# A decoder block on one core: where the low halves of weights are made, and Silu in one operation

## The chip, the cores and the metric

The kernel runs on one core of a Trainium2 chip. The metric is the time of one execution on the device in microseconds (us). Before the change it is 1216.52 us, the median of three runs (1215.63 to 1218.12). A further execution was recorded by the hardware profiler; all rows of the trace come from that one.

## The reference

One layer, 1024 tokens, width 1024, everything float32. `x` is normalised and modulated, one big projection gives eight parts, two branches use them, and gates merge the branches:

```python
mod = jax.nn.silu(c) @ w_ada + b_ada
shift, scale, gate = jnp.split(mod, 3, axis=-1)
h = rms_norm(x, norm_gain) * (1.0 + scale[:, None, :]) + shift[:, None, :]
q, k, v, z_a, u, z_b, m_a, m_b = jnp.split(h @ w_in, offs, axis=-1)
attn = stick_breaking_attention(to_heads(q), to_heads(k), to_heads(v))
p_a = (attn * jax.nn.silu(z_a)) @ w_branch_a
pooled = multiscale_causal_pool(u, pool_w, pool_scale)
p_b = (pooled * jax.nn.silu(z_b)) @ w_branch_b
merged = jax.nn.sigmoid(m_a) * p_a + jax.nn.sigmoid(m_b) * p_b
return x + gate[:, None, :] * (merged @ w_out)      # then a last rms_norm
```

The attention has 16 heads of 64; its weights are products of sigmoids over the keys, not a softmax. The pooling takes trailing means over 2, 4, 8 and 16 tokens, minus the token itself. Silu is a number times its sigmoid. It occurs three times that matter here: on `z_b` (the pooling branch's gate), on `z_a`, and on `c`, whose product with the last third of `w_ada` gives the output gate.

## The kernel before

**Halves.** Every operand of a big matmul is split in two: a high half, rounded to the matmul's input format (a copy on ScalarE), and a low half, the difference (a subtraction, mostly on VectorE). A product of two operands is three matmuls: high by high, high by low, low by high. Making halves is therefore a large part of the work of ScalarE and VectorE. `split` (L119) and `load_w` (L134) load a weight tile and make both halves on arrival.

**Tiles of weights made ahead.** The last big stage, attention, projects 40 tiles of `w_in` (keys, queries, `z_a` of eight pairs of heads, and 16 tiles of the merge gates) in the order of the list `tiles`. The first `PLAIN` = 8 are split on arrival: ScalarE makes the high half, GpSimd the low half (VectorE for tile 4). For the other 32 the low half is made in earlier stages and kept in DRAM, in `wl_d`. That is `make_lo(pl, n, bufs, later)` (L147): for each of `n` tiles it takes a buffer `lraw` from pool `pl`, loads the weights into it (L154), copies the high half into the single buffer `lhi` on ScalarE (L157), subtracts it in place on VectorE (L158), and stores the buffer to `wl_d` (L159). The text calls one such step a low part. In attention `load_parts` (L167) loads such a tile twice, the weights and the stored low half, and ScalarE copies the high half (L174).

**Stages in order.**
1. Statistics of `x`, the modulation, the transposed and modulated input `hT`, and the projection `u` with the pooling map already multiplied in (matmuls named wm, ua, u), up to 128.6 us.
2. The values `v` (128.6 to 215.6 us): sixteen blocks of 24 matmuls; each result is split (L614, L615) and stored to `v_d` (L616). In the sequence of `u`, eight low parts; after each value block `LO_V` says how many more, ten in all, with the two steps of one apart by a block (`later`). Four of the eight pooling differences (`make_d`) are made here too.
3. The gate's stage (from 215.6 us): for each of eight tiles of `z_b`, two halves of 24 matmuls each (10.89 us a tile), then `silu`: ScalarE writes the sigmoid to `gb` (L668), VectorE multiplies it by `z_b` (L669) and by the pooling difference and its scale (L670). The sums `t1`, `t2` of parts of `gb` are taken (L674 to L677). Here the low parts by `LO_ZB`, four in all, and the output gate: `c` is spread to all partitions, ScalarE takes its sigmoid into `gjunk`, VectorE multiplies (L683), and for each of eight tiles of `w_gate` a load (L685) and a product with a sum (L686). Buffers `lraw`, three of them, serve the low parts, `gjunk` and `w_gate` in turn. All lie in pool `pb`, which is open for this stage and the next.
4. The seven products (to 396.9 us): `gb` times `w_branch_b` as a two by two block product with seven multiplications instead of eight, p1, p5, p6, p7, p4, p3, p2. Each takes two pairs of operands: a weight block `a` (loaded at L653, some of them sums of blocks) and a block of `gb` or of `t1`, `t2`, both split (L658 and L659, L646 and L647). The second load buffer `ar` and the results lie in pool `sums`. That pool opens when `diffs` closes, that is, on the space of the pooling differences, after the last of them has been read at L670. After each product `LO_PB` low parts, ten in all, with buffers in `pb`.
5. Attention with the forty projections between its steps (396.9 to about 1036 us), then `w_branch_a`, the merge and `w_out` to the end. Here the order of the matmuls is written out by hand and pinned. GpSimd masks the blocks on the diagonal (L936) for VectorE's running products (L938).

**What sets the order.** In stages 2 to 4 nothing is pinned. A planner places the instructions on each engine's queue, and the DMAs on SP's, by its own modelled times: an instruction may go ahead of others that stand before it in the program, as soon as its inputs and a free buffer allow. On the chip each queue then runs strictly in the planned order, and an instruction that waits holds all behind it. Weight tiles have two buffers for the loaded tile (`raw`) and two for its halves (`whl`); matmul results have eight PSUM banks.

Of the kernel before, what the change touches and what calls it, by code (L numbers as in the profile page):

```python
# [9 lines left out]
F32 = mybir.dt.float32  # L10
F32R = mybir.dt.float32r
AF = mybir.ActivationFunctionType
# [3 lines left out]
P = 128  # L16
D = 1024
# [16 lines left out]
NWT = 4  # L34


PLAIN = 8

MASKED = 4
LO_V = (1, 0, 1, 1, 0, 1, 1, 0)  # L40
LO_ZB = (0, 1, 0, 1, 0, 1, 0, 1)
LO_PB = (1, 2, 1, 2, 1, 2, 1)

DIFFS = {1: 0, 4: 1, 7: 2, 10: 3}
HD = 64
# [12 lines left out]
def block_kernel(ctx, tc, a, out):  # L58
    nc = tc.nc
    v, act, gp = nc.vector, nc.scalar, nc.gpsimd  # L60

    def pool(name, **kw):
        return tc.tile_pool(name=name, bufs=1, reuse_waits="tile", **kw)
# [9 lines left out]
    def bank(tag, name):  # L73
        return psp.tile([P, 512], F32, tag=tag, bufs=BANKS[tag], name=name)
# [3 lines left out]
    def any_bank(name):  # L78
        return bank(next(turns), name)
# [54 lines left out]
    def load_w(src, name, hi_eng, lo_eng):  # L134
        raw = wts.tile([P, KB, P], F32, tag="raw", bufs=2, name=name + "_raw")
        nc.sync.dma_start(raw.rearrange("p k c -> p (k c)"), src)
        return split(raw, [P, KB, P], wts, "whl", 2, hi_eng, lo_eng, name)
# [6 lines left out]
    tiles += gates  # L144
    early_lo = iter(range(PLAIN, len(tiles)))

    def make_lo(pl, n, bufs=3, later=False):  # L147

        rest = []
        for _ in range(n):  # L150
            i = next(early_lo)
            raw = pl.tile([P, D], F32, tag="lraw", bufs=bufs, name=f"l{i}_raw")
            hi = pl.tile([P, D], F32R, tag="lhi", bufs=1, name=f"l{i}_hi")
            nc.sync.dma_start(raw, a["w_in"][tiles[i]])  # L154

            def low(i=i, raw=raw, hi=hi):
                act.copy(hi, raw)  # L157
                v.tensor_sub(raw.bitcast(F32R), raw, hi.bitcast(F32))  # L158
                nc.sync.dma_start(wl_d[i], raw)  # L159

            if later:
                rest.append(low)
            else:
                low()
        return rest

    def load_parts(i, name):  # L167
        if i < PLAIN:
            return load_w(a["w_in"][tiles[i]], name, act, v if i == MASKED else gp)
        raw = wts.tile([P, KB, P], F32, tag="raw", bufs=2, name=name + "_raw")  # L170
        nc.sync.dma_start(raw.rearrange("p k c -> p (k c)"), a["w_in"][tiles[i]])
        hl = wts.tile([P, 2, KB, P], F32R, tag="whl", bufs=2, name=name)
        nc.sync.dma_start(hl[:, 1].rearrange("p k c -> p (k c)").bitcast(F32), wl_d[i])
        act.copy(hl[:, 0], raw)  # L174
        return hl[:, 0], hl[:, 1]
# [17 lines left out]
    def project(ct, name, use, he, le):  # L193
        whl = load_w(a["w_in"][ct], name, he, le)
        for sh in range(2):
            ps = any_bank(f"{name}_{sh}")
            mm3(ps, whl, (h_hi, h_lo), range(KB), hmov(sh))
            use(sh, ps)
# [18 lines left out]
    with pool("init") as init:  # L217
# [101 lines left out]
        wg, maps, halves = {}, {}, {}  # L319
# [223 lines left out]
        for i in range(NA, KB):  # L543
            ps = bank("pj", f"u{i}_0")
# [14 lines left out]
    def load_u(j):  # L559
        u = dif.tile([P, S + 16], F32, tag="u", bufs=2, name=f"u{j}")  # L560
        v.memset(u[:, S:], 0.0)
        nc.sync.dma_start(u[:, :S], u_d[j])
        return u

    def make_d(j, u):
        win = WINDOWS[j // 2]
        cur, n, step = u, S + 16, 1
        while step < win:
            nxt = dif.tile([P, S + 16], F32, tag="win", bufs=2, name=f"win{j}_{step}")
            n -= step  # L570
            v.tensor_add(nxt[:, :n], cur[:, :n], cur[:, step:step + n])
            cur, step = nxt, 2 * step
        t0 = S - win + 1
        d = dif.tile([P, S], F32, tag="d", bufs=5, name=f"d{j}")
        v.scalar_tensor_tensor(d[:, :t0], cur[:, :t0], 1.0 / win, u[:, :t0], ALU.mult, ALU.subtract)
        tl = dif.tile([P, 16], F32, tag="tl", bufs=2, name=f"tl{j}")
        v.tensor_mul(tl[:, :win - 1], cur[:, t0:S], invn[:, 16 - win + 1:])
        v.tensor_sub(d[:, t0:], tl[:, :win - 1], u[:, t0:S])
        dhls[j] = d


    with pool("vp") as vp:
# [6 lines left out]
        for i in reversed(range(KB)):  # L589
            ps = any_bank(f"u{i}_1")  # L590
# [9 lines left out]
        for hf in range(2):  # L600
            if hf == 0:
                wv.append([load_wv(1, k2) for k2 in range(4)])
            for sb in range(8):
                ss = slice(sb * P, (sb + 1) * P)
                ps = any_bank(f"v{sb}_{hf}")
# [14 lines left out]

                now, todo = todo, make_lo(vp, LO_V[sb], later=True)
                if 8 * hf + sb in DIFFS:
                    j = DIFFS[8 * hf + sb]
# [8 lines left out]
    pb = pbs.enter_context(pool("pb"))  # L632
# [6 lines left out]
    sg = pb.tile([P, D], F32, name="sg")  # L639
# [4 lines left out]
    def b_op(src, name):  # L644
        hl = pb.tile([P, 2, 2, 512], F32R, tag="bhl", bufs=3, name=name)
        act.copy(hl[:, 0], src)  # L646
        v.tensor_sub(hl[:, 1], src, hl[:, 0].bitcast(F32))  # L647
        return hl
# [7 lines left out]
    def a_op(src, name):  # L656
        hl = wts.tile([P, 2, 2, 512], F32R, tag="whl", bufs=2, name=name)
        act.copy(hl[:, 0], src)  # L658
        v.tensor_sub(hl[:, 1], src, hl[:, 0].bitcast(F32))  # L659
        return hl  # L660

    for j in range(KB):
        if j not in dhls:
            make_d(j, load_u(j))

        def silu(sh, ps):
            z = gb[:, j, sh * 512:sh * 512 + 512]
            act.activation(z, ps, AF.Sigmoid)  # L668
            v.tensor_mul(z, ps, z)  # L669
            v.scalar_tensor_tensor(z, dhls[j][:, sh * 512:sh * 512 + 512], psc_v[:, j:j + 1], z, ALU.mult, ALU.mult)  # L670

        project(CZB + j, f"wzb{j}", silu, act, v)
        if j < 4:
            v.tensor_sub(t1[:, j], gb[:, j, 512:], gb[:, j, :512])  # L674
        else:
            v.tensor_sub(t2[:, j - 4], gb[:, j, 512:], t1[:, j - 4])
            v.tensor_sub(gb[:, j - 4, 512:], gb[:, j, 512:], gb[:, j - 4, 512:])  # L677
        make_lo(pb, LO_ZB[j])
        if j == 0:
            nc.sync.dma_start(sg, a["c_row"].broadcast_to([P, D]))  # L680
            gjunk = pb.tile([P, D], F32, tag="lraw", bufs=3, name="gjunk")
            act.activation(gjunk, sg, AF.Sigmoid)
            v.tensor_mul(sg, sg, gjunk)  # L683
        wg = pb.tile([P, D], F32, tag="lraw", bufs=3, name=f"wg{j}")
        nc.sync.dma_start(wg, a["w_gate"][j])  # L685
        v.scalar_tensor_tensor(wg, wg, 1.0, sg, ALU.mult, ALU.mult, accum_out=gate[:, j:j + 1])  # L686
        del dhls[j]
# [4 lines left out]
    sums = pbs.enter_context(pool("sums", side="right"))  # L692
# [48 lines left out]
    def copied(tag, bufs, j, src):  # L741
        t = sums.tile([P, 512], F32, tag=tag, bufs=bufs, name=f"{tag}_{j}")
        act.copy(t, src)
        return t
# [5 lines left out]
    for n, (name, a_of, b_of) in enumerate(products):  # L750
        c = {"p5": "b", "p3": "b", "p2": "c"}.get(name, "a")
        if c not in chain:
            chain[c] = [bank((tb if c == "b" else ta)[j], f"{name}_{j}") for j in range(4)]
        ps = chain[c]
        for q in range(2):
            wl_, ml_ = a_op(a_of(q), f"{name}a{q}"), b_op(b_of(q), f"{name}b{q}")
            for j in range(4):
                for e in range(2):
                    for i, (w, m) in enumerate(((0, 0), (0, 1), (1, 0))):
                        mm(  # L760
                            ps[j], wl_[:, w, e, j * P:(j + 1) * P], ml_[:, m, e],
                            start=name in ("p1", "p5", "p2") and (q, e, i) == (0, 0, 0), stop=(q, e, i) == (1, 1, 2),
                                skip_group_check=True,
                        )
        for j in range(4):
            if name == "p1":
                keep["s1", j] = copied("s1", 4, j, ps[j])
            elif name == "p6":
                keep["s2", j] = copied("s2", 4, j, ps[j])
            elif name == "p7":  # L770
                out_b(j + 4, 1, added(copied("s3", 2, j, ps[j]), chain["b"][j]))
            elif name == "p4":
                out_b(j + 4, 0, copied("s4", 2, j, ps[j]))
            elif name == "p3":
                out_b(j, 1, added(keep["s2", j], ps[j]))
            elif name == "p2":
                out_b(j, 0, added(keep["s1", j], ps[j]))
        make_lo(pb, LO_PB[n])
    pbs.close()


# [295 lines left out]
    with pool("fin") as fin:  # L1077
# [14 lines left out]
        for sh in range(2):  # L1092
            sl = slice(sh * 512, sh * 512 + 512)
            ms = []
            for j in range(KB):
# [8 lines left out]
                ps = bank("pj", f"pa{sh}_{j}")  # L1104
                n = 0
# [12 lines left out]
            for i in range(4):  # L1118
# [8 lines left out]
                for c_, cl in enumerate(pieces):  # L1127
                    w_ = cl.stop - cl.start
                    ps = bank(("z", "tr")[c_ % 2], f"o{sb}_{c_}")[:, :w_]
                    n = 0  # L1130
# [85 lines left out]
```

## Time and profile before

| what | value |
|---|---|
| median of three runs | 1216.52 us (1215.63 to 1218.12) |
| the profiled execution | 1219.61 us |
| its span, first to last instruction | 1217.9 us |
| TensorE busy | 1194.0 us, 98% |
| VectorE busy | 796.7 us, 65% |
| ScalarE busy | 549.9 us, 45% |
| GpSimd busy | 167.9 us, 14% |
| moved by DMA | 212.39 MB |

How to read it: engines are PE (TensorE matmuls), PEld (its weight loads), DVE (VectorE), ACT (ScalarE), POOL (GpSimd) and SP (the queue that issues DMAs). A row of the timeline gives start, duration, engine, line, operation, the tile written and the tiles read, shape and count; in brackets stands how long the engine was idle before, and what ended that. A row of a group gives the count, the busy time, the mean in ns, and after the bar the idle time before such instructions and its causes. The chain of waits is followed back from the last instruction to what released it, step by step. A window's row gives each engine's busy time in that stretch, and then the granted clock of TensorE as a share of full speed.

### The profile page before, as it was taken

How to read it: one execution, taken by the hardware profiler on the slowest of the kernel's cores; microseconds unless marked ns; L12 is line 12 of the kernel's file. 1: busy time of each engine (PE TensorE's matmuls, PEld its weight loads, DVE VectorE, ACT ScalarE, POOL GpSimd, SP SyncE). 2: the span in 40 equal slices, each digit the busy share in tenths (PEclk: the TensorE clock that was granted, in tenths of full speed). 3: DMA queues.
4: the chain of work that ended last, by engine and by line, in shares of the span. 5: the costliest groups of instructions: out<-in, count | busy, mean ns of one | idle time of the engine just before them, and what ended most of it. 6: DMA issues, size and time to landing. Idle time of an engine off the chain costs nothing.

```text
span 1217.9 us, 16134 instructions
## 1 busy us (share of the span) xinstructions
PE 1194.0 (98%) x5698; PEld 995.8 (82%) x5698; DVE 796.7 (65%) x1088; ACT 549.9 (45%) x1020; POOL 167.9 (14%) x352
## 2 busy tenths in 40 slices
PE   8999999999699999999999999999999999999997
PEld 7888888887488888888888888888888888888886
DVE  5754591686675186777768678687777753795643
ACT  5564331332453255655656555555655653232211
POOL 1000000000000333222222221222221210000001
PEclk9999999999899999999999999999999999999999
DMA  9649994767735732343534325353353335985622
GB/s 350 259 168 360 308 380 169 231 221 166 271 138 178 224 92 70 107 135 104 162 116 138 101 95 164 110 155 99 110 143 100 96 123 173 352 273 168 208 72 84
DMA packets 85699, 212.39 MB, mean 174 GB/s; under 512 B 10609, under 2 KB 24049, under 8 KB 83442
## 3 DMA queue, kind: packets, MB, share of 16 engines
q1 hardware_dynamic: 77410, 196.47, 49.8%
q10 hardware_dynamic: 8208, 14.88, 3.3%
q8 instruction: 45, 0.74, 0.3%
q14 instruction: 36, 0.29, 0.1%
HBM read 144.20 MB, written 50.34 MB: 160 GB/s over the span
## 4 chain that ended last, share of the span: by engine, by line
PE 82%; DMA 7%; DVE 5%; issue 4%; ACT 1%; POOL 0%; SPq 0%; POOLq 0%; ACTq 0%; DVEq 0%
PE p L108 38%; PE v L108 7%; PE o L108 6%; PE z L108 6%; PE av L108 5%; PE wt L108 5%; PE pa L108 5%; PE u L108 4%; DMA wl_d<-l_raw 3%; PE ua L108 3%; DMA l_raw<-in_w_in 1%; PE wm L108 1%; DMA m<-sb_d 1%; PE wzb L108 1%; DMA kh<-kh 1%
## 5 line engine op out<-in xcount | busy, mean ns | idle before, releaser
L108 PE MATMUL p<-hT,w 128*128 128x512 f32 x1920 | 480.1, 391 | 0.6 <-ACT m_sg L203 0.6
L108 PEld LDWEIGHTS p<-hT,w 128*128 128x128 f32 x1920 | 355.2, 188 | 74.8 <-ACT m_sg L203 1.0
L938 DVE TENSOR_TENSOR_SCAN om<-om 128x512 f32<-128x512 f32 (+7 forms) x128 | 175.7, 1373 | 124.7 <-ACT om L931 69.1
L931 ACT ACTIVATE om<-z 128x512 f32<-128x512 f32 (+2 forms) x192 | 94.5, 492 | 156.4 <-PE z L108 133.9
L957 ACT CAST wt<-wt 128x512 fp32r<-128x512 f32 (+1 forms) x160 | 88.2, 551 | 48.2 <-PE wt L108 47.9
L958 DVE TENSOR_TENSOR wt<-wt,wt 128x512 fp32r<-128x512 f32 (+1 forms) x160 | 99.2, 620 | 16.2 <-ACT wt L957 15.6
L108 PE MATMUL av<-wt,vv 128*128 128x512 f32 x320 | 106.4, 414 | 0.0
L936 POOL TENSOR_SCALAR_AFFINE_SELECT om<-om 128x128 f32<-128x128 f32 x128 | 56.4, 441 | 346.9 <-ACT om L931 287.5
L108 DVE TENSOR_TENSOR be<-be,om 128x511 f32<-128x511 f32 (+7 forms) x128 | 95.1, 748 | 1.1 <-POOL be L936 0.7
L932 ACT ACTIVATE be<-z 128x512 f32<-128x512 f32 (+2 forms) x192 | 94.1, 490 | 0.0
L108 PE MATMUL pa<-ga,wa 128*128 128x512 f32 x384 | 89.9, 390 | 0.7 <-DVE s L1110 0.6
L108 PE MATMUL o<-wo,mhl 128*128 128x512 f32 (+1 forms) x408 | 89.6, 377 | 0.0
L108 PE MATMUL wzb<-hT,wzb 128*128 128x512 f32 x384 | 87.6, 390 | 2.0 <-DVE wzb L123 2.0
L108 PE MATMUL wt<-ident,be 128*128 128x128 f32 x576 | 89.4, 273 | 0.0
L108 PE MATMUL v<-wv,hT 128*128 128x512 f32 x384 | 87.2, 389 | 0.0
L108 PEld LDWEIGHTS wzb<-hT,wzb 128*128 128x128 f32 x384 | 71.9, 188 | 17.5 <-DVE wzb L123 2.5
L108 PEld LDWEIGHTS pa<-ga,wa 128*128 128x128 f32 x384 | 71.9, 188 | 16.4 <-issue 1.0
L108 PEld LDWEIGHTS o<-wo,mhl 128*128 128x128 f32 x408 | 73.5, 188 | 14.1
L108 PEld LDWEIGHTS v<-wv,hT 128*128 128x128 f32 x384 | 72.1, 188 | 14.9
L108 PEld LDWEIGHTS wt<-ident,be 128*128 128x128 f32 x576 | 70.2, 141 | 11.6
L157 ACT CAST l_hi<-l_raw 128x1024 fp32r<-128x1024 f32 x32 | 33.6, 1051 | 72.6 <-DMA l_raw<-in_w_in 54.8
L158 DVE TENSOR_TENSOR l_raw<-l_raw,l_hi 128x1024 fp32r<-128x1024 f32 x32 | 39.1, 1222 | 41.7 <-ACT l_hi L157 41.6
(175 smaller groups left out, 1481.8 us busy)
## 6 DMA issues: line engine op xcount, KB each, us to landing
w_raw<-in_w_in SPq DMA_DIRECT2D x40, 512.0 KB, 4.6
l_raw<-in_w_in SPq DMA_DIRECT2D x32, 512.0 KB, 4.9
wl_d<-l_raw SPq DMA_DIRECT2D x32, 512.0 KB, 5.9
w<-wl_d SPq DMA_DIRECT2D x32, 512.0 KB, 4.0
v_d<-vo SPq DMA_DIRECT2D x16, 512.0 KB, 5.2
vv<-v_d SPq DMA_DIRECT2D x8, 1024.0 KB, 5.3
wa_raw<-in_w_branch_a SPq DMA_DIRECT2D x16, 512.0 KB, 4.8
wa<-in_w_mod SPq DMA_DIRECT2D x7, 1024.0 KB, 6.3
```

Of the source, the lines that this page charges most:

```text
L108: ins = op(*args, **kw)
L157: act.copy(hi, raw)
L158: v.tensor_sub(raw.bitcast(F32R), raw, hi.bitcast(F32))
L931: act.activation(om[:, b0:b0 + n], zp[:, :n], AF.Sigmoid, scale=-0.125)
L932: act.activation(be[:, b0:b0 + n], zp[:, :n], AF.Sigmoid, scale=0.125)
L936: gp.affine_select(out=tl[:, :P], in_=tl[:, :P], pattern=[[1, P]], compare_op=ALU.is_gt, fill=fill, base=0, channel_multiplier=-1)
L938: v.tensor_tensor_scan(om[:, :W], om[:, :W], om[:, :W], 1.0, ALU.mult, ALU.min)
L957: act.copy(wt[:, 0, :off], pt[:, :off])
L958: v.tensor_sub(wt[:, 1, :off], pt[:, :off], wt[:, 0, :off].bitcast(F32))
```

## The change

Three things. First, the low parts: `PLAIN` goes from 8 to 10, so that 30 low parts are left; the values' blocks take 14 instead of 10, the gate's stage none instead of 4, the products 8 instead of 10. The products' low parts get their buffers in `sums`, two instead of three `lraw`. Second, `w_gate` gets one buffer of its own, `wg`, in place of a turn in `lraw`. Third, ScalarE writes Silu itself, of `z_b` and of `c`, and VectorE's multiplications at L669 and L683 go.

```diff
-PLAIN = 8
+PLAIN = 10
...
-LO_V = (1, 0, 1, 1, 0, 1, 1, 0)
-LO_ZB = (0, 1, 0, 1, 0, 1, 0, 1)
-LO_PB = (1, 2, 1, 2, 1, 2, 1)
+LO_V = (1, 1, 1, 1, 1, 1, 1, 0)
+LO_PB = (0, 2, 1, 2, 1, 1, 1)
...
             z = gb[:, j, sh * 512:sh * 512 + 512]
-            act.activation(z, ps, AF.Sigmoid)
-            v.tensor_mul(z, ps, z)
+            act.activation(z, ps, AF.Silu)
             v.scalar_tensor_tensor(z, dhls[j][:, sh * 512:sh * 512 + 512], psc_v[:, j:j + 1], z, ALU.mult, ALU.mult)
...
-        make_lo(pb, LO_ZB[j])
         if j == 0:
             nc.sync.dma_start(sg, a["c_row"].broadcast_to([P, D]))
-            gjunk = pb.tile([P, D], F32, tag="lraw", bufs=3, name="gjunk")
-            act.activation(gjunk, sg, AF.Sigmoid)
-            v.tensor_mul(sg, sg, gjunk)
-        wg = pb.tile([P, D], F32, tag="lraw", bufs=3, name=f"wg{j}")
+            act.activation(sg, sg, AF.Silu)
+        wg = pb.tile([P, D], F32, tag="wg", bufs=1, name=f"wg{j}")
         nc.sync.dma_start(wg, a["w_gate"][j])
...
-        make_lo(pb, LO_PB[n])
+        make_lo(sums, LO_PB[n], 2)
```

## The prediction

> **What bounds the kernel now.** I read the page first, then the waits of TensorE, its timeline around the one place where it stands still, the windows there, and the chain that ended last.
>
> ```profile
> span 1217.9 us, 16134 instructions
> ```
> ```profile
> 294.38 10.73 PE L108 MATMUL wzb<-hT,wzb 128*128 128x512 f32 x46 [2.04 <-DVE wzb L123]
> 310.05 1.22 PE L108 MATMUL p<-p1b,p1a 128*128 128x512 f32 x2 [4.94 <-ACT p1a L658]
> 311.61 6.71 PE L108 MATMUL p<-p1b,p1a 128*128 128x512 f32 x22 [0.34 <-DVE p1a L659]
> 321.88 7.22 PE L108 MATMUL p<-p1b,p1a 128*128 128x512 f32 x24 [3.56 <-ACT p1a L658]
> 330.85 11.28 PE L108 MATMUL p<-p5b,p5a 128*128 128x512 f32 x48 [1.74 <-ACT p5a L658]
> 341.97 11.15 PE L108 MATMUL p<-p6b,p6a 128*128 128x512 f32 x48
> 352.95 11.15 PE L108 MATMUL p<-p7b,p7a 128*128 128x512 f32 x48
> ...
> 396.90 25.37 PE L108 MATMUL p<-hT,w 128*128 128x512 f32 x111
> ```
> ```profile
> 190.00:200.00 10.00, 10.00 (x46) 8.29 (x45) 0.71 (x2) 1.18 (x2) 0.00 (x0) 1.00 0.31 111
> ...
> 290.00:300.00 10.00, 7.96 (x35) 6.09 (x35) 7.85 (x10) 3.10 (x5) 0.00 (x0) 1.00 0.67 190
> 300.00:310.00 10.00, 5.11 (x23) 3.91 (x21) 3.29 (x4) 3.52 (x4) 0.00 (x0) 0.89 0.84 286
> 310.00:320.00 10.00, 7.93 (x24) 5.61 (x24) 7.32 (x9) 3.24 (x4) 0.00 (x0) 0.77 0.92 338
> 320.00:330.00 10.00, 7.22 (x24) 5.50 (x24) 7.28 (x8) 4.20 (x7) 0.00 (x0) 0.83 0.62 236
> ...
> 440.00:460.00 20.00, 20.00 (x104) 16.90 (x103) 17.91 (x22) 12.83 (x27) 5.92 (x11) 1.00 0.45 105
> ```
> The columns of a window are TensorE, its weight loads, VectorE, ScalarE, GpSimd, the granted clock, the share of the DMA engines and GB/s. TensorE is full in the values' stage (190) and in attention (440); between 292 and 331 it waits five times, 2.04 + 4.94 + 0.34 + 3.56 + 1.74 = 12.62 us. Besides, the clock fell to 0.89, 0.77 and 0.83 there: 0.51 of 10 us is 5.1 us of clock withheld, part of it while TensorE stood idle anyway.
>
> What the place costs in all follows from the pitch of the work. The chain has the start of the gate's stage and, further on, what held it:
> ```profile
> 215.64 10.89 PE wzb L108 x48
> ...
> 271.70 13.11 DMA wl_d<-l_raw
> 284.83 4.17 DMA l_raw<-in_w_in
> ```
> A gate tile takes 10.89 us, a product 352.95 - 341.97 = 10.98. Eight tiles from 215.64 end at 302.76, seven products at 379.62. The projections start at 396.90, so **17.28 us** are lost in the two stages, by idleness and clock together. That is the most that the change can win here, and elsewhere TensorE has no wait worth naming.
>
> The cause stands on ScalarE:
> ```profile
> 307.52 1.04 ACT L157 CAST l_hi<-l_raw 128x1024 fp32r<-128x1024 f32 x1 [4.96 <-DMA l_raw<-in_w_in]
> 308.48 0.59 ACT L668 ACTIVATE gb<-wzb 128x512 f32<-128x512 f32 x1
> 308.96 1.03 ACT L658 CAST p1a<-a 128x1024 fp32r<-128x1024 f32 x1
> ```
> ```profile
> L157 ACT CAST l_hi<-l_raw 128x1024 fp32r<-128x1024 f32 x7 | 7.3, 1048 | 32.1 <-DMA l_raw<-in_w_in 29.4 <-DVE wzb L123 2.8
> L668 ACT ACTIVATE gb<-wzb 128x512 f32<-128x512 f32 x5 | 3.0, 590 | 0.0
> ```
> The second fence groups 285 to 325 us. ScalarE runs its queue in order. The copy of a low part (L157) waits 4.96 us for its weights; behind it stand the gate's sigmoid and p1's operand, for which TensorE waits 4.94. Seven such copies wait 32.1 us. Their weights are late because a buffer comes free only when its low part has been stored: the chain's 13.11 us store, then the next load.
>
> **The change, part by part.**
>
> *Low parts out of the gate's stage.* The planner may run a low part ahead of its place in the program as soon as a buffer is there.
> ```profile
> L158 DVE TENSOR_TENSOR l_raw<-l_raw,l_hi 128x1024 fp32r<-128x1024 f32 x14 | 17.1, 1220 | 22.4 <-ACT l_hi L157 22.4
> ...
> L669 DVE TENSOR_TENSOR gb<-wzb,gb 128x512 f32<-128x512 f32 x16 | 10.9, 682 | 5.2 <-ACT gb L668 5.2
> ```
> From 215 to 335 all fourteen low parts of the two stages ran, the products' ten among them: their buffers lay in a pool that was open from the gate's first tile. Now four go to the values, two are dropped, and the eight left use a pool that opens only when the pooling differences have been read, so nothing can be drawn ahead into the gate's stage. With them go each one's load and store from SP's queue. All of the 17.28 us stood behind them: minus 17.28.
>
> *Four more in the values' stage.* Each brings 1.05 us on ScalarE, 1.22 on VectorE, a load and a store. The row at 190 shows 0.71 of 10 us of VectorE and 0.31 of the DMA engines used, and TensorE can run on over eight PSUM banks of 5.44 us. Cover enough: 0. Without it each costs at most a copy's mean wait, 32.1/7 = 4.6 us.
>
> *Eight in the products.* A cycle of a buffer is load, copy, subtraction, store:
> ```profile
> l_raw<-in_w_in SPq DMA_DIRECT2D x32, 512.0 KB, 4.9
> wl_d<-l_raw SPq DMA_DIRECT2D x32, 512.0 KB, 5.9
> ```
> 4.9 + 1.05 + 1.22 + 5.9 = 13.1 us, by two buffers one low part in 6.5 us; eight need 52 of the products' 77 us. But a copy that waits holds the operand copies behind it:
> ```profile
> 347.66 1.05 ACT L658 CAST p7a<-a11d 128x1024 fp32r<-128x1024 f32 x1 [3.50 <-PE p L108]
> ```
> This operand could begin at 347.66, its low half ends 1.05 + 1.22 later at 349.93, and p7 starts at 352.95: a cover of 3.0 us. A copy's wait of 4.6 exceeds it by 1.6. Two such operands fall into a product's 11 us, and a wait hurts if it begins in the last 1.6 us ahead of one: 8 x 2 x 1.6/11 = 2.3 of the eight. I take two at the full 1.6: **plus 3.2 us**. Bounds: 0, and all eight, 12.8. Gaps this short should leave the clock alone: the wait of 2.04 us at 294 left it at 1.00.
>
> *p1 to p5.* p5's second operand is loaded only after the last difference is read:
> ```profile
> 323.31 0.74 DVE L670 SCALAR_TENSOR_TENSOR gb<-d,vecs,gb 128x512 f32<-128x512 f32 x1
> ```
> From there to p5's start at 330.85 is 7.54 us. Afterwards this read comes about 302.76 + 0.59 = 303.35, p5 can start at 310.89, and p1 keeps TensorE until 313.74: hidden, with 2.85 us to spare.
>
> *Silu in one operation.* It takes sixteen multiplications of 0.68 us and one of 1.22 off VectorE, 12.1 us, and shortens the way from PSUM to p5. No Silu stands in the trace; the nearest row is the sigmoid at 0.59 us, and ScalarE is busy 4.20 of 10 us at most in the windows above, so double would be hidden as well, and half would gain nothing: 0. It needs another table than the sigmoid. A table change in this trace:
> ```profile
> 12.10 1.28 ACT L108 ACT_TABLE_LOAD   x1
> 13.39 1.09 ACT L108 ACTIVATE sigb<-crow 128x512 f32<-128x512 f32 x2
> ```
> 1.28 us, and the sigmoid follows within 0.01. Two changes are added, at the gate's start and here:
> ```profile
> 423.20 0.60 ACT L931 ACTIVATE om<-z 128x512 f32<-128x512 f32 x1 [2.76 <-PE z L108]
> ```
> ScalarE idles 2.76 us ahead of the first sigmoid of attention, so both are hidden: 0; uncovered, 2.6. The Trainium skill (ScalarE: Activation LUTs, "What ACT_TABLE_LOAD costs") counts about 2.66 us a change, with a drain of 1.38 that this trace does not show, and advises against mixing sets; by it the uncovered cost is 5.3, and covered, which 2.76 just allows, it is 0 too.
>
> *Two more plain tiles.* Tiles 8 and 9 (pair 2's query tile and a gate tile) get their low part from GpSimd during attention, and two loads, two copies and two stores vanish:
> ```profile
> 448.62 2.40 POOL L123 TENSOR_TENSOR w<-w_raw,w 128x1024 fp32r<-128x1024 f32 x1 [6.03 <-ACT w L128]
> 450.97 0.30 POOL L936 TENSOR_SCALAR_AFFINE_SELECT om<-om 128x128 f32<-128x128 f32 x1
> ```
> 2.40 us twice on GpSimd; the mask behind it started at once, and TensorE is full in that window (20.00 of 20). 0; uncovered, 4.8.
>
> *w_gate's own single buffer.* SP holds a load until the previous product has read the buffer. A turn is some 4.9 + 1.22 = 6.1 us of the tile's 10.89: 0.
>
> **Sum.** -17.28 + 3.2 = -14.1. The profiled execution, 1219.61 us (span 1217.9 and 1.7 around it), becomes 1205.5. It lay 3.1 above the median of the three runs; from the median 1216.52 comes **1202.4 us**. The best case, from the fastest run 1215.63 with no rest, is 1198.3; with all eight copies at the full rest of 12.8, 1212.0.
>
> **The rivals.**
>
> *The wait moves to p5.* Two low parts' loads get ahead of p5's in SP's queue as the new pool opens: 2 x 4.9 - 2.85 = 6.95 us, with the clock in the present ratio (17.28/12.62 = 1.37) 9.5, so 1208.7. The Trainium skill (TensorE: Matmul & The Clock Gate, "The HAM clock gate") has the clock fall to half after an idle window of 3.4 us and stay there for as long; by that two gaps of about 3.5 would add 1.7 each, 10.4 in place of 9.5. For it: both share queue and pool, and p5's own wait of 1.74 was a load's. Against: in the program they stand behind p5.
>
> *Slower: ScalarE's blockade moves whole into the products.* There too the low parts may be drawn together, now over two buffers instead of three, right behind p1. At the present price of 17.28/7 = 2.47 each, eight cost 19.8 us: 1216.5 - 17.3 + 19.8 = 1219.0. It decides once the copies wait 3.0 + 2.2 = 5.2 us on average, as two of the present did. Against it: 52 us of cycle in 77, and DMA engines no longer shared with the gate's loads.
>
> *No change: SP's queue was the cause.* If w_gate's single buffer holds the queue more than 10.89 - 6.1 = 4.8 us a tile, the gate's weights and p1's operands behind it come as late as now: 1216.5. Against: VectorE loses 12.1 us of multiplications and fourteen subtractions, and reads at once.
>
> **How the numbers follow.** The forecast, with a rest of 0 to 6 us, 0.67; the wait at p5 0.17; no change 0.09; slower 0.07. Three runs spread over 0.2%, so that is what a measurement can tell from none. Faster is 0.67 + 0.17 = 0.84. The range 1198.3 to 1212.0 holds the first two, some 0.83.
>
> **What would show it.** Right: between the gate's start and the first projection some 167 us instead of 181; no low part's subtraction between 216 and 303, four more before; two more table loads; VectorE's busy time down by about 14.5 us, GpSimd's up by 4.8; clock 1.00 at 300 to 330. Wrong: operand copies of p5 or p6 behind waiting low-part copies, TensorE idle over 6 us in the products, or its first projection later than 390 us.

## The result and the profile after

The changed kernel takes 1205.39 us (median of four runs, 1204.15 to 1206.92), the kernel before 1216.41 beside it. The ratio is 0.991, with a 95% interval of 0.9894 to 0.9925: 11.0 us faster, where 14.1 were forecast. The profiled execution took 1204.15 us, the fastest of the four, with a span of 1202.4; that of the kernel before, 1219.61, lay above all of its other executions there. So the two profiles lie further apart (15.5 us of span) than the medians.

The page of the changed kernel, busy times:

```profile
span 1202.4 us, 16106 instructions
...
PE 1189.3 (99%) x5698; PEld 993.1 (83%) x5698; DVE 786.8 (65%) x1069; ACT 550.5 (46%) x1020; POOL 172.2 (14%) x354
```

TensorE's timeline of the changed kernel from the end of the gate's stage to the first projection (the changed file is shorter, so that its line numbers are one lower than before up to the gate's stage and five lower behind it):

```profile
283.62 18.52 PE L107 MATMUL wzb<-hT,wzb 128*128 128x512 f32 x81
301.98 11.17 PE L107 MATMUL p<-p1b,p1a 128*128 128x512 f32 x48
312.99 7.49 PE L107 MATMUL p<-p5b,p5a 128*128 128x512 f32 x32
...
334.96 11.15 PE L107 MATMUL p<-p7b,p7a 128*128 128x512 f32 x48
347.83 3.95 PE L107 MATMUL p<-p4b,p4a 128*128 128x512 f32 x16 [1.72 <-ACT s L738]
352.07 7.67 PE L107 MATMUL p<-p4b,p4a 128*128 128x512 f32 x32 [0.29 <-DVE p4a L658]
360.44 11.28 PE L107 MATMUL p<-p3b,p3a 128*128 128x512 f32 x48 [0.70 <-ACT p3a L657]
371.56 11.15 PE L107 MATMUL p<-p2b,p2a 128*128 128x512 f32 x48
382.54 25.70 PE L107 MATMUL p<-hT,w 128*128 128x512 f32 x111
```

The waits of 2.04, 4.94, 3.56 and 1.74 us ahead of p1 and p5 are gone. New ones of 1.72, 0.29 and 0.70 stand at p4 and p3. The first projection starts at 382.54 instead of 396.90. The clock stays up (windows of the changed kernel, same columns as before):

```profile
300.00:310.00 10.00, 10.00 (x45) 8.21 (x44) 6.76 (x8) 3.85 (x5) 0.00 (x0) 1.00 0.64 234
310.00:320.00 10.00, 10.00 (x45) 8.22 (x44) 8.44 (x9) 7.06 (x10) 0.00 (x0) 1.00 0.86 305
320.00:330.00 10.00, 10.00 (x46) 8.19 (x45) 10.00 (x10) 5.02 (x6) 0.00 (x0) 1.00 0.74 249
```

What is left comes from ScalarE (timeline of the changed kernel):

```profile
346.25 1.04 ACT L156 CAST l_hi<-l_raw 128x1024 fp32r<-128x1024 f32 x1 [3.36 <-DMA l_raw<-in_w_in]
347.20 1.07 ACT L738 COPY s<-p 128x512 f32<-128x512 f32 x2
...
353.32 2.20 ACT L738 COPY s<-p 128x512 f32<-128x512 f32 x4 [0.86 <-DMA pb_d<-s]
358.85 0.59 ACT L738 COPY s<-p 128x512 f32<-128x512 f32 x1 [3.33 <-DMA pb_d<-s]
359.33 1.05 ACT L657 CAST p3a<-a12s 128x1024 fp32r<-128x1024 f32 x1
```

A low part's copy waits 3.36 us for its weights, and behind it stand the copies that empty p7's banks, for which p4 waits. Then ScalarE waits 3.33 us for a result buffer that has not been stored, and p3's operand stands behind that.

### The profile page after: what moved, and what is told of

It reads as the page before. It is cut to its first block, busy times and chain, and to the rows that moved or that the text cites. A ratio compares the mean times of both kernels' runs of the same rounds, so it can differ in the third digit from the quotient of the medians.

```text
span 1202.4 us, 16106 instructions
## 1 busy us (share of the span) xinstructions
PE 1189.3 (99%) x5698; PEld 993.1 (83%) x5698; DVE 786.8 (65%) x1069; ACT 550.5 (46%) x1020; POOL 172.2 (14%) x354
## 4 chain that ended last, share of the span: by engine, by line
PE 93%; DMA 3%; DVE 1%; issue 1%; ACT 1%; SPq 0%; POOL 0%; POOLq 0%; ACTq 0%; DVEq 0%
PE p L107 41%; PE wzb L107 7%; PE v L107 7%; PE pa L107 7%; PE o L107 6%; PE z L107 6%; PE av L107 6%; PE wt L107 5%; PE u L107 5%; PE ua L107 3%; DMA wa<-in_w_mod 1%; PE wm L107 1%; DMA wt<-in_w_ut 1%; DMA pb_d<-s 1%; DMA wl_d<-l_raw 0%
## 5 line engine op out<-in xcount | busy, mean ns | idle before, releaser
L933 DVE TENSOR_TENSOR_SCAN om<-om 128x512 f32<-128x512 f32 (+7 forms) x128 | 177.5, 1387 | 124.9 <-ACT om L926 69.0
L107 PEld LDWEIGHTS o<-wo,mhl 128*128 128x128 f32 x408 | 73.5, 188 | 14.1
L122 POOL TENSOR_TENSOR w<-w_raw,w 128x1024 fp32r<-128x1024 f32 x9 | 22.2, 2465 | 345.9 <-ACT w L127 345.9
L107 PE MATMUL z<-kl,q 128*128 128x512 f32 (+2 forms) x192 | 65.5, 341 | 0.0
```

The source lines that it names most:

```text
L107: ins = op(*args, **kw)
L122: lo_eng.tensor_tensor(lo, src, hi.bitcast(F32), op=ALU.subtract)
L933: v.tensor_tensor_scan(om[:, :W], om[:, :W], om[:, :W], 1.0, ALU.mult, ALU.min)
```

## The experiments

The theory at first (A): the low parts that the planner drew into the gate's stage held ScalarE, and with it TensorE. The rivals were B (VectorE's relief by Silu made the gain) and C (buffers shared with `w_gate`). Twelve runs were made in three groups, each group beside the kernel before, which gave 1216.3, 1217.6 and 1217.2 us.

**e1, the low parts alone.** The changed kernel, with the old way of Silu:

```diff
-            act.activation(z, ps, AF.Silu)
+            act.activation(z, ps, AF.Sigmoid)
+            v.tensor_mul(z, ps, z)
```

(`c` goes back to sigmoid and multiplication in the same way; its sigmoid takes the buffer `wg`.)

> The changed kernel with the sigmoid and the multiplications as before (ScalarE writes the sigmoid, VectorE multiplies, 16 x 0.68 + 1.22 = 12.1 us of VectorE put back); c's sigmoid goes into the one buffer of w_gate. Theory A, the low parts that were drawn into the gate's stage held ScalarE and with it TensorE: all of the gain stays, 1204 to 1207 us, from the gate's start to the first projection some 167 to 168 us as in the changed kernel (167.4), no second pair of table loads. Rival B, VectorE's relief made the gain: it falls away, 1211 us or more, that stretch 173 us or more.

Measured: 1207.82 us, ratio 0.9927 (0.9915 to 0.9939). The first projection starts at 383.56. Most of the gain is there without Silu. It is slightly above the range expected; its interval overlaps the changed kernel's.

**e2, Silu alone.**

```diff
-            act.activation(z, ps, AF.Sigmoid)
-            v.tensor_mul(z, ps, z)
+            act.activation(z, ps, AF.Silu)
```

(The same for `c`.)

> The kernel before with Silu in one operation alone; low parts and buffers as before. Theory A: nothing to measure, 1214.5 to 1217 us, TensorE still waits over 9 us for p1's operands (12.6 before in all). Rival B, VectorE at 10 of 10 from 230 to 280 delayed the low parts, so that its relief of 12.1 us frees the stage: 1205 to 1210 us.

Measured: 1207.26 us, ratio 0.9922 (0.991 to 0.9934). Theory A as stated is wrong: with all fourteen low parts at their old places in the program, Silu alone takes 9.0 us. TensorE's timeline of this kernel:

```profile
293.32 0.73 PE L108 MATMUL wzb<-hT,wzb 128*128 128x512 f32 x2 [1.53 <-ACT wzb L128]
294.95 10.74 PE L108 MATMUL wzb<-hT,wzb 128*128 128x512 f32 x46 [0.90 <-DVE wzb L123]
305.52 0.62 PE L108 MATMUL p<-p1b,p1a 128*128 128x512 f32 x2
306.91 7.14 PE L108 MATMUL p<-p1b,p1a 128*128 128x512 f32 x30 [0.76 <-DVE p1a L659]
```

But B alone does not stand either, since e1 does without Silu. Two edits that each bring nearly the whole are not two causes; they shorten the same thing. The candidate is the end of the series of low parts. Of the subtractions (line, engine, operation, count, durations in ns, start of the first and of the last) the kernel before and e2 have:

```profile
L158 DVE TENSOR_TENSOR l_raw<-l_raw,l_hi x32: 1200/1225/1227, 93.5 to 320.4; 128x1024 fp32r<-128x1024 f32 x32
```
```profile
L158 DVE TENSOR_TENSOR l_raw<-l_raw,l_hi x32: 1214/1224/1227, 93.5 to 309.2; 128x1024 fp32r<-128x1024 f32 x32
```

The last one comes 11.2 us earlier, about what Silu takes off VectorE (12.1); against another execution of the kernel before (316.6, e8 below) it is 7.4. VectorE was nearly full where the series ran (windows of the kernel before, columns as in the prediction):

```profile
230.00:240.00 10.00, 10.00 (x46) 8.29 (x45) 10.00 (x15) 4.13 (x5) 0.00 (x0) 1.00 0.85 287
240.00:250.00 10.00, 10.00 (x46) 8.29 (x45) 7.37 (x10) 0.96 (x2) 0.00 (x0) 1.00 0.59 203
250.00:260.00 10.00, 10.00 (x46) 8.29 (x45) 9.28 (x14) 4.58 (x7) 0.00 (x0) 1.00 0.76 273
260.00:270.00 10.00, 10.00 (x46) 8.29 (x45) 10.00 (x14) 4.53 (x6) 0.00 (x0) 1.00 0.60 206
270.00:280.00 10.00, 10.00 (x46) 8.29 (x45) 10.00 (x13) 3.78 (x5) 0.00 (x0) 1.00 0.96 143
```

That VectorE's relief is what moved the series is argued from this, not shown apart: with Silu the planner also put ScalarE's and SP's instructions of this stage in another order.

The gate's stage ends at 302.7. In the kernel before, ScalarE's copy of p1's second operand stands right behind the last low part's (320.80 behind 319.36), so that p1 cannot go on until the series is through. A late low part ahead of 302.7 costs little (here 1.53 + 0.90 us for a weight tile of the gate), one behind it holds TensorE.

**e3, drawing ahead allowed again.** The changed kernel with the products' low parts in the pool that is open from the gate's stage on:

```diff
-        make_lo(sums, LO_PB[n], 2)
+        make_lo(pb, LO_PB[n], 2)
```

> The changed kernel with one thing undone: the products' eight low parts take their two buffers from the pool that is open from the gate's stage on, so that the planner can draw them ahead. Theory A1, the stage broke because there were more low parts than buffer turns: eight by 13.1/2 us are 52 us, done by about 275 of 302, no wait there and none later in the products: 1201 to 1205 us. Theory A2, low parts in the gate's stage hold its ScalarE whatever their number: 8/14 of the 17.3 us lost come back, 1211 to 1214 us.

Measured: 1201.60 us, ratio 0.9878 (0.9866 to 0.9891), 3.8 us less than the changed kernel. The series and TensorE's first projection in this kernel:

```profile
L157 DVE TENSOR_TENSOR l_raw<-l_raw,l_hi x30: 1215/1224/1227, 94.5 to 271.1; 128x1024 fp32r<-128x1024 f32 x30
```
```profile
379.67 20.61 PE L107 MATMUL p<-hT,w 128*128 128x512 f32 x90
```

A1 holds and A2 falls. Drawing these eight into the gate's stage is harmless, and better than making them in the products; the series ends in time.

**e4, a buffer of its own for `w_gate`.** The kernel before with this edit (c's sigmoid takes the same buffer):

```diff
-        wg = pb.tile([P, D], F32, tag="lraw", bufs=3, name=f"wg{j}")
+        wg = pb.tile([P, D], F32, tag="wg", bufs=1, name=f"wg{j}")
...
-        make_lo(pb, LO_ZB[j])
+        make_lo(pb, LO_ZB[j], 2)
...
-        make_lo(pb, LO_PB[n])
+        make_lo(pb, LO_PB[n], 2)
```

> The kernel before with one edit: w_gate and c's sigmoid get one buffer of their own, and the low parts of gate and products two instead of three. Rival C, turns shared with w_gate made the low parts late: 1205 to 1211 us. Theory A1: fourteen low parts by two buffers at 13.1/2 us are 92 us from 219, past the gate's end as before: 1214 to 1222 us, TensorE's waits ahead of p1 and p5 at 10 us or more.

Measured: 1213.33 us (1209.16 to 1217.22), ratio 0.9969 (0.9957 to 0.9982), between the two. The last subtraction comes at 318.8, and TensorE waits 6.68 us for p1's operand. With this edit the low parts also have two buffers where they shared three, so that it does not show what sharing alone cost; a buffer for `w_gate` in this form is worth 3.0 us.

**e5, the gate vector in larger packets.** Something else stretched the series. The chain's store of 13.11 us in the kernel before has a neighbour: SP issues the store of the output gate, 1024 numbers, at 271.2, half a microsecond ahead of it. DMA issues of that line, kernel before:

```profile
L689 SPq DMA_DIRECT2D g_d<-gate x1: 385/385/385, 271.2 to 271.2; - x1
...
DMA to landing us min/median/max: 12.8/12.8/12.8
```

4 KB in 1024 packets of 4 bytes need 12.8 us, and while they are under way the low part's 512 KB beside them need 13.1 instead of a median of 5.9. Dealt to partitions in another order, the gate's numbers lie together by eights:

```diff
-    nc.sync.dma_start(g_d[0].rearrange("(k p) -> p k", p=P), gate)
+    nc.sync.dma_start(g_d[0].rearrange("(p k) -> p k", p=P), gate)
...
-        "w_gate": np.ascontiguousarray(wm[:, 2 * D:].T).reshape(KB, P, D),
+        "w_gate": np.ascontiguousarray(wm[:, 2 * D:].T.reshape(P, KB, D).transpose(1, 0, 2)),
```

(The bias of the gate is reordered in the same way.)

> The kernel before with one edit: the gate's 1024 numbers go to DRAM as 128 packets of 32 bytes instead of 1024 of 4 (rows of w_gate and of its bias dealt to partitions in another order); in the kernel before this 4 KB store took 12.8 us to land, from 271 to 284, and a low part's store beside it 13.1. Theory D, the fourteen low parts are a series with a deadline at the gate's end, and whatever takes some 10 us out of it frees the stage: last subtraction of the series at 309 to 314 instead of 320, 1206 to 1212 us. Rival B2, VectorE alone sets the pace of the series (10 of 10 until 282): nothing gained, 1215 to 1217 us.

Measured: 1209.53 us, ratio 0.9935 (0.9922 to 0.9948), 8.1 us less than the kernel before. The same line and the series in this kernel:

```profile
L689 SPq DMA_DIRECT2D g_d<-gate x1: 382/382/382, 268.4 to 268.4; - x1
...
DMA to landing us min/median/max: 5.6/5.6/5.6
```
```profile
L158 DVE TENSOR_TENSOR l_raw<-l_raw,l_hi x32: 1214/1225/1228, 93.3 to 310.2; 128x1024 fp32r<-128x1024 f32 x32
```

The low part's store beside it, issued 0.7 us behind, in this kernel:

```profile
L159 SPq DMA_DIRECT2D wl_d<-l_raw x1: 326/326/326, 269.1 to 269.1; - x1
...
DMA to landing us min/median/max: 6.0/6.0/6.0
```

It lands in 6.0 us instead of 13.1 (12.2 when the kernel before ran again). This is the cleanest of the tests: from 85 to 400 us ScalarE and SP have the same instructions in the same order as in the kernel before. Theory D, the series with a deadline, holds: a third thing that has to do with neither Silu nor the number of low parts gives most of the gain by ending the series 10.2 us earlier (6.4 against the other execution of the kernel before). B2 falls.

**e6, all low parts with the values.**

```diff
-LO_V = (1, 1, 1, 1, 1, 1, 1, 0)
-LO_PB = (0, 2, 1, 2, 1, 1, 1)
+LO_V = (2, 1, 2, 1, 2, 1, 2, 0)
+LO_PB = (0,) * 7
```

> The changed kernel with the products' eight low parts made with the values too (22 there, 30 in all), none in the gate's stage or the products. Theory A1: thirty by three buffers at 13.1/3 us are 131 us, from 90 to some 221, so that neither the gate's stage nor the products hold any: 1200 to 1204 us, TensorE without a wait from 215 to the first projection. Rival E, the values' stage, whose DMA engines are full from 130 to 190, is overfilled: values' results or the gate's first weights come late, TensorE waits between 190 and 230, 1205 us or more.

Measured: 1206.29 us (1204.78 to 1207.85), ratio 0.9913 (0.9898 to 0.9928). A1's time is missed; E's time came, but not its cause. The values' stage is not overfilled, TensorE waits nowhere from 190 to 300. The series ends at 240.6, later than the 221 worked out. But TensorE waits 1.41 us at p5 and 0.60 at p6, since VectorE waits 4.59 us, until 310.88, for one of p5's first pair of blocks. That load was issued at 299.46, half a microsecond behind the gate vector's store (298.99, 11.2 us to land):

```profile
L652 SPq DMA_DIRECT2D a<-in_w_branch_b x1: 577/577/577, 299.5 to 299.5; - x1
...
DMA to landing us min/median/max: 11.3/11.3/11.3
```

In the changed kernel, where that store was issued at 261.6, the same load took 5.7 us. It looks like the small packets again, now in the way of a load; no run takes them out of this kernel to show it. Why other runs are up to 3 us above the profiled one (1204.78) stays open.

**e7 and e8, both kernels once more.**

> The changed kernel once more. If the profiled execution was typical, TensorE's waits in the products are 2 to 4 us again, the stretch from the gate's start to the first projection 167 to 169 us, and the median 1204 to 1206.5 us; if it was a lucky one, waits of 4 to 8 us and that stretch 169 to 172 us.

> The kernel before once more, one look. If the wait for p1's operands differs from execution to execution, the stretch from the gate's start to the first projection is 176 to 180 us here instead of 181.3, with the whole execution shorter by as much (1215 to 1218 us); if it is fixed, 181 us again.

Measured: the changed kernel again 1205.09 us, ratio 0.9905 (0.9891 to 0.9918), 12.5 us below the kernel before beside it. The profiled execution (1206.83 us) shows the same waits at p4 and p3, 2.84 us in all, the first projection at 382.74, and a new one after it: 1.68 us at 395.49, released by VectorE's subtraction for the keys. So executions of the changed kernel differ behind the products. The kernel before, once more, took 1214.56 us; its timeline of TensorE:

```profile
306.19 0.73 PE L108 MATMUL p<-p1b,p1a 128*128 128x512 f32 x2 [3.65 <-ACT p1a L658]
307.76 6.76 PE L108 MATMUL p<-p1b,p1a 128*128 128x512 f32 x22 [0.83 <-DVE p1a L659]
318.05 7.20 PE L108 MATMUL p<-p1b,p1a 128*128 128x512 f32 x24 [3.53 <-ACT p1a L658]
326.99 7.61 PE L108 MATMUL p<-p5b,p5a 128*128 128x512 f32 x32 [1.74 <-ACT p5a L658]
...
393.67 8.57 PE L108 MATMUL p<-hT,w 128*128 128x512 f32 x37
```

The stall is 3.2 us shorter here than in the execution on which the prediction was built (393.67 against 396.90), and the last subtraction comes at 316.6 instead of 320.4. The loss is not a constant: it follows the series' end.

**e9, Silu and the gate vector together,** all low parts as in the kernel before (the edits of e2 and e5).

> The kernel before with two edits that leave all low parts where they were: Silu in one operation, and the gate's numbers in 128 packets. Alone they took 9.0 and 8.0 us. Theory D, a series with a deadline: with Silu the last subtraction came at 309.2, and 6 us earlier it meets the gate's end at 302.7, so that what is lost shrinks to the operands' own waits of 1 to 4 us: 1201 to 1205 us, less than the sum. Rival, the gains simply add: 1199.5 us or less.

Measured: 1201.23 us, ratio 0.9871 (0.9855 to 0.9887). This beats the changed kernel without moving one low part. The series and the timeline of TensorE:

```profile
L158 DVE TENSOR_TENSOR l_raw<-l_raw,l_hi x32: 1216/1225/1227, 93.4 to 300.9; 128x1024 fp32r<-128x1024 f32 x32
```
```profile
302.46 11.17 PE L108 MATMUL p<-p1b,p1a 128*128 128x512 f32 x48
313.46 11.15 PE L108 MATMUL p<-p5b,p5a 128*128 128x512 f32 x48
...
379.38 22.88 PE L108 MATMUL p<-hT,w 128*128 128x512 f32 x100
```

The last subtraction comes just ahead of the gate's end, and no wait is left. The two edits gave 9.0 and 8.1 alone and 16.0 together. That lies between the plain sum, 17.1, and the expected saturation, and cannot tell them apart.

**e10 to e12, variants of e3:** with the gate vector of e5, without Silu, and with `PLAIN` = 8 and `LO_PB` = (1, 2, 1, 2, 1, 2, 1).

> The kernel of the third run (products' low parts drawn ahead, 1201.6 us, no wait between the gate's start and the projections) with the gate's numbers in 128 packets. Theory D: the series there ended at 271, far from its deadline, nothing is left to gain, 1200.5 to 1202.5 us. If the small packets cost in themselves: 1199 us or less.

> The kernel of the third run with sigmoid and multiplications as before. Theory D: VectorE's 12.1 us move the series' end from 271 to some 283, still ahead of 302, 1201 to 1203 us, no wait in that stretch. Rival B: Silu's relief is needed whatever the low parts do, 1206 us or more.

> The kernel of the third run with eight plain tiles as before and so ten low parts in the products instead of eight. Theory D: two turns of 6.5 us move the series' end to some 284, 1201 to 1203 us; the two plain tiles in attention cost nothing and bring nothing. If the plain tiles in attention cost GpSimd's 4.8 us: 1197 to 1199 us; if they carry a gain: 1205 us or more.

Measured: 1200.87 (0.9869, 0.9854 to 0.9884), 1201.37 (0.9873, 0.9857 to 0.9889) and 1203.22 us (0.9901, 0.9882 to 0.992). Once the series ends early, Silu and the gate vector bring nothing that can be measured. In e3 the gate vector's store is issued at 278.7, behind the last low part, so that there was nothing for it to hold up. In e11 the series ends at 274.7, only 3.6 us later than in e3 and not the 12 expected: what VectorE's 12.1 us are worth to the series depends on the arrangement. Without the two plain tiles the series ends at 289.5 and TensorE waits 0.89 us once in the gate's stage; the median lies a little above the range expected, and its runs spread from 1201.89 to 1208.01, for which no run shows a reason.

All kernels in one table, from the profiled execution of each (us):

| kernel | last low part's subtraction | first projection | median |
|---|---|---|---|
| before | 320.4 | 396.90 | 1216.4 |
| before again (e8, one run) | 316.6 | 393.67 | 1214.6 |
| own buffer (e4) | 318.8 | 391.75 | 1213.3 |
| gate vector (e5) | 310.2 | 388.05 | 1209.5 |
| Silu (e2) | 309.2 | 386.04 | 1207.3 |
| Silu and gate vector (e9) | 300.9 | 379.38 | 1201.2 |
| no plain tiles (e12) | 289.5 | 380.10 | 1203.2 |
| open pool without Silu (e11) | 274.7 | 378.87 | 1201.4 |
| open pool and gate vector (e10) | 273.2 | 379.48 | 1200.9 |
| open pool (e3) | 271.1 | 379.67 | 1201.6 |
| all with the values (e6) | 240.6 | 381.91 | 1206.3 |
| changed | 353.1, in the products | 382.54 | 1205.4 |
| changed again (e7) | 353.1, in the products | 382.74 | 1205.1 |
| low parts alone (e1) | 354.5, in the products | 383.56 | 1207.8 |

Among those that make the low parts ahead of the products, the first projection comes later by about as much as the series runs past 302 (by 17 us for 18, 14 for 15, 8.5 for 8; with the own buffer less, 12 for 17). e6 is the exception: its series ends first of all, and yet it is slower than e3, at p5 and, by its median, at a place that was not found. In the changed kernel the last eight are spread over the products and cost 2.7 us there.

## Why the prediction was right, and where it was not

**The place and the wait: right.** The stretch between the gate's start and the first projection takes 382.54 - 215.10 = 167.4 us, forecast some 167; it was 181.3. That is 13.8 of the 15.5 us between the two profiled executions. No low part's subtraction stands between 208 and 311, four more stand before. The waits ahead of p1 and p5 went with the low parts, and the clock with them.

**Minus 17.28: mis-sized for the median.** This is the step that made the sum too large. It took the loss of one profiled execution, which lay 3.1 us above the median, from the median. The same kernel again lost 3.1 us less in that stretch (393.67 - 215.51 = 178.2 us). e3, which has no wait there, is 14.7 us below the kernel before beside it (1216.3 and 1201.6); e9 and e10 are 16.0 and 16.4 below theirs. So the median's loss was some 15 to 16 us, and the term was 1 to 2.6 too large. Together with the next step this covers the distance from the 14.1 forecast to the 11.0 and 12.5 measured; it divides the measured times and does not check them. Profile against profile the sum looks better, 1205.5 forecast and 1204.15 measured, but there luck helped: the one execution was among the longest of its kernel, the other among the shortest.

**Plus 3.2 for the low parts in the products: right in size, partly another wait.** TensorE waits 1.72 + 0.29 + 0.70 = 2.71 us there, and e3, where these low parts run earlier, has a stretch 3.6 us shorter (379.67 - 215.87 = 163.8) and a median 3.8 us lower. That two of eight copies would each cost 1.6 us was a choice within 0 to 12.8, and that the size came out so near it is partly luck. The prediction saw ScalarE's operand copies behind a waiting copy. At p4 it was the emptying of the banks, and at p3 ScalarE waited for a store of results.

**The cause: too narrow.** "Seven such copies wait 32.1 us" because of a 13.11 us store was read rightly, but taken as the ordinary price of a low part. The store was slow because 1024 packets of 4 bytes ran beside it (e5), and the series was late also because VectorE was busy for 46.7 of the 50 us from 230 to 280 (argued, see e2). "All of the 17.28 us stood behind them" fits the runs; that moving them was the only thing in the change that could win it back does not.

**Silu at 0: right beside the rest, wrong as a price of the edit.** Alone it takes 9.0 us. In the changed kernel it adds some 2.4 (e1 against the changed kernel, with intervals that overlap), and in e3's arrangement nothing (e11). The prediction counted its 12.1 us of VectorE as covered, and asked only whether TensorE waits for VectorE, not whether VectorE paces the low parts for which it waits. (ScalarE's "4.20 of 10 us at most" holds for the rows up to 330; in the row at 440 it is 12.83 of 20, where this edit adds nothing but the table change.)

**"Nothing can be drawn ahead into the gate's stage", and p5's loads after the last difference: wrong, without effect.** SP issued p5's first two blocks and two low parts' loads at 295.6 to 297, ahead of the last difference read at 302.81; so the space that they use was free by then. Nor is drawing ahead a fault in itself (e3).

**The rest.** The values' stage took its four low parts without a wait, as forecast: the stage's last four subtractions came at 185.5 to 205.8, all but the first in the slack end that the row at 190 shows. Ahead of it that row does not hold; in the kernel before the DMA engines were full from 140 to 190 (shares of 0.99 to 1.05). The two table changes came, and cost what the row of before shows (timeline of ScalarE, changed kernel):

```profile
217.24 1.28 ACT L678 ACT_TABLE_LOAD   x1 [1.51 <-DMA sg<-in_c_row]
218.54 1.06 ACT L678 ACTIVATE sg<-sg 128x1024 f32<-128x1024 f32 x1
```

Nothing waits for either; the second, at 406.43, lies ahead of a wait for TensorE. The drain of 1.38 us that the Trainium skill (ScalarE: Activation LUTs, "What ACT_TABLE_LOAD costs") adds does not show here either: the Silu starts 0.02 us after the load, the second load within 0.02 us of the copy ahead of it, and the measurement decides. GpSimd's busy time rose by 4.3 us, forecast 4.8; VectorE's fell by 9.9, forecast 14.5; attention's running products took up 1.8 us of the difference (175.7 before, 177.5 after), the rest was not followed. None of the three rivals came: p5 waits for nothing in the changed kernel, the blockade did not move whole, and `w_gate`'s single buffer held nobody.

## What to carry to other kernels

Work that runs beside the bound engine can have a deadline rather than a price. Ask when its last piece must be done and what sets the pace of the series; then edits that have nothing else in common each win back what they take off the overrun, and once the series ends in time a further one wins nothing. Tests of one edit alone show each as "the cause". Before subtracting a stall from a median, see how far the profiled execution lies from that median, since a stall of this kind differs from execution to execution.

## What the runs showed that was not expected

A store of 4 KB can hold up stores of half a megabyte. In packets of 4 bytes it took 12.8 us in the kernel before and 9.5 to 14.6 in other kernels; in packets of 32 bytes 5.6, 4.4 and 1.4 (e5, e9, e10). The low part's store beside it took 13.1 us in the kernel before and 6.0 in e5. There, that alone was worth 8.1 us.
